# Attention of a hybrid encoder layer as a longer software pipeline, with half of the sample units transposed on TensorE

## The chip, the cores and the metric

The kernel runs on one core of one Trainium2 chip. The metric is the device time of one execution in microseconds (us). Engines: PE is TensorE (matmuls; PEld its weight loads), DVE is VectorE, ACT is ScalarE, POOL is GpSimd, SP is SyncE, which only issues DMAs here.

## The reference, cut to what matters

One encoder layer is applied to two token groups (256 prompt and 1024 sample tokens) that share their weights: a mixer of grouped-query attention and a gated linear recurrence (HGRN2), then cross-attention to a memory, then an MLP. The change touches the attention of the mixer alone. T is 256 or 1024, there are 8 query heads on 2 key/value heads, 64 numbers each:

```python
def blocked_gqa_attention(q, k, v):          # q (B,T,8,64), k and v (B,T,2,64)
    ...
    def attend(qblk):                        # one block of 128 queries
        s = jnp.einsum('bkgqd,bksd->bkgqs', qblk, kh).astype(jnp.float32) * scale
        p = jax.nn.softmax(s, axis=-1).astype(vh.dtype)
        return jnp.einsum('bkgqs,bksd->bkgqd', p, vh)
...
merged = jax.nn.sigmoid(gate_a) * (o_a @ w_pa) + jax.nn.sigmoid(gate_b) * (o_b @ w_pb)
return merged @ w_out                        # then layer norm, cross-attention, MLP
```

## The kernel before

The phases follow one another: keys and values of the memory, the recurrence (`hgrn`), the projections `qkv`, `attention`, and then `back` for each half of the tokens, which begins with the merge of the two branches and needs the attention's output. To keep precision every fp32 operand of a matmul is a high and a low part, so that a product takes two or three matmuls.

`attention` works in 68 **units**, in this order: 64 of the sample group (one head, 128 queries, 1024 keys each; two units in a row, `qt` 0 and 1, make up one head's 256 queries), then 4 of the prompt group (four heads, 128 queries, 256 keys each). Inside the loop over `x` (a **step**) one operation of several units is written out, and within `tc.manual_schedule` PE, ACT and DVE run their instructions in just the order in which the code gives them. POOL and SP get theirs from a scheduler. For one sample unit:

- `scores`: four matmuls (L437, L438) into a PSUM tile `S`, of which there are two;
- `row_max` (L443, DVE), then `exps` (L451, ACT), which writes the unnormalised weights `pr` (three buffers in turn) and their sums `sm`;
- `recip` (L456 and L457, DVE): 1/sum, with a factor `PS`;
- the weights must be normalised, split into two f16 parts, and transposed, so that keys lie on partitions. For two units in three the DMA transposes: `dma_hi` (L464, ACT) writes the high part into `p16`, `dma_lo` (L469, DVE) the low part, and SP issues a transposing DMA (L471). Every third sample unit (`on_pe`, 21 of the 64) goes by TensorE instead: POOL normalises (L561), `pe_turn` makes eight transposes into the one PSUM tile `T` (L477), ACT copies the high part from it (L570), DVE subtracts for the low part (L571);
- `weigh`: 16 matmuls with the values for two units of a head (L490, called PV below), in two pieces of eight, then the **eviction** of the PSUM tile `of` by ACT into `oev` (L494), and a DMA to DRAM. One piece is issued a step, `PVLAG` steps after the unit.

Into the same loop a **filler** is woven: 144 pieces of three matmuls (L116 to L118) that project gates needed later, two or three a step. Eight pieces fill one `of` tile, which ACT copies to `gev` (L630) and POOL's queue stores. PV and filler share the two `of` tiles (pool `psV`). The filler's weights are loaded by SP, and split by ACT (L86, "weight cast" below) and POOL (L87).

The prompt units have no PE transposes. Behind the last unit come the last PVs, their stores (`oa_d<-oev`, two `oev` buffers), the loads `y<-oa_d` in `back` (L729) and their split (L86), for which the merge's matmuls wait. Meanwhile PE does matmuls of `back` that need no attention (`a<-act,w`).

Of the kernel before, what the change touches and what calls it, by code (L numbers as in the profile page):

```python
# [10 lines left out]
F32 = mybir.dt.float32  # L11
# [3 lines left out]
AF = mybir.ActivationFunctionType  # L15
ALU = mybir.AluOpType
# [4 lines left out]
P = 128  # L21
# [5 lines left out]
KT = D // P  # L27
HD = 64
# [10 lines left out]
GRP = T // 2  # L39
GCH = [(0, 256), (256, 384)]  # L40
# [18 lines left out]
W8E = (0, 1, 0, 1)  # L59
PORD = 64  # L60
PVS = 1
PVLAG = 5
PEVERY = 3
VS = 1024.0
PS = 32768.0


class Kern:
# [340 lines left out]
    def attention(self, ap, psS, psT, psV, fills):  # L409
        nc = self.nc  # L410
        SC = 256
        aw = self.t(self.actp, [P, 10240], F32, "act")
        cnt = {"pt": 0, "pr": 0}

        def new_pt(m):
            i = cnt["pt"] % 4
            cnt["pt"] += 1
            return aw[:, i * 2048:(i + 1) * 2048].bitcast(F16).rearrange("p (j a s q) -> p j a s q", j=2, a=m, q=SC)

        def new_pr(m):  # L420
            i = cnt["pr"] % 3
            cnt["pr"] += 1
            x = self.t(ap, [P, 1024], F32, "prx", 1) if i == 2 else aw[:, 8192 + i * 1024:9216 + i * 1024]
            return x.rearrange("p (a s) -> p a s", a=m)


        def scores(u):
            si, kv, hs, t0 = u[:4]
            s0, s1 = SEQS[si]
            L = (s1 - s0) * P  # L430
            n = min(512, L)
            S = self.t(psS, [P, 1024], F32, "S")
# [21 lines left out]
        def recip(u, sm):  # L454
            m = len(u[2])
            nc.vector.tensor_scalar(sm[:, :m], sm[:, :m], 1.0 / PS, None, op0=ALU.mult)  # L456
            nc.vector.reciprocal(sm[:, :m], sm[:, :m])  # L457
# [9 lines left out]
        def dma_lo(u, pr, sm, p16, dst):  # L467
            for a in range(len(u[2])):
                nc.vector.scalar_tensor_tensor(p16[:, 1, a], pr[:, a], sm[:, a:a + 1], p16[:, 0, a],  # L469
                                               op0=ALU.mult, op1=ALU.subtract)  # L470
            nc.sync.dma_start_transpose(out=dst.rearrange("p j a s q -> p (j a s) q"), in_=p16.rearrange("p j a s -> p (j a s)"))  # L471


        def pe_turn(pr):
            pt = self.t(psT, [P, 8, P], F32, "T")
            for j in range(8):
                nc.tensor.transpose(pt[:, j], pr[:, 0, j * P:(j + 1) * P], self.ident)  # L477
            return pt

        def weigh(si, h0, c0, pts):  # L480

            s0, s1 = SEQS[si]
# [12 lines left out]
            if m == 2:  # L495
                for j in range(2):
                    nc.sync.dma_start(self.oa_d[j, h0 // 2, :, :, c0:c0 + SC].rearrange("h d t -> d h t"), os_[j * HD:(j + 1) * HD])
            else:
                nc.sync.dma_start(self.oa_d[:, h0 // 2, h0 % 2, :, c0:c0 + SC], os_[:, 0])

        units = []

# [15 lines left out]
        pvs = []  # L518

        def slot(x):  # L520
            u = units[x]
            if u[4] == 0:
                u[5][0] = new_pt(len(u[2]))
            return u[5][0][:, :, :, :, u[4] * P:(u[4] + 1) * P]

        def close(x):
            si, kv, hs, t0, qt, pts, c0 = units[x]
            if qt:
                k = min(2, len(hs))
                pvs.extend((x, weigh(si, hs[a], c0, [pts[0][:, :, a + y] for y in range(k)])) for a in range(0, len(hs), k))  # L530

        def step_pv(x, k):
            while k > 0 and pvs and pvs[0][0] <= x - PVLAG:
                if next(pvs[0][1], 0) == 0:
                    pvs.pop(0)
                else:
                    k -= 1

        keys = [("wga" if g[0] == 0 else "wgb", g[1]) for g in fills]

        def feed():
            for i, g in enumerate(fills):
                if i + 1 < len(fills):
                    self.w_ahead(keys[i + 1])
                yield from self.gate(*g, psV, "of", self.evp)
# [5 lines left out]
        for x in range(n + PVLAG + 3):  # L551
# [4 lines left out]
            y, z = x - 1, x - 2  # L556
            if 0 <= y < n:
                recip(units[y], R[y][1])
                if on_pe[y]:
                    pr, sm = R[y]  # L560
                    nc.gpsimd.tensor_scalar(pr, pr, sm[:, 0:1], None, op0=ALU.mult)  # L561
            if 0 <= z < n and not on_pe[z]:
                dma_lo(units[z], *R.pop(z), H.pop(z), slot(z))
                close(z)
            if x + 1 < n:
                M[x + 1] = row_max(units[x + 1], S[x + 1])
            if 0 <= z < n and on_pe[z]:
                pt = pe_turn(R.pop(z)[0])
                dst = slot(z)
                nc.scalar.copy(dst[:, 0, 0], pt)  # L570
                nc.vector.tensor_tensor(dst[:, 1, 0], pt, dst[:, 0, 0], op=ALU.subtract)  # L571
                close(z)
            if 0 <= y < n and not on_pe[y]:
                H[y] = dma_hi(units[y], *R[y])
# [4 lines left out]
        assert not pvs  # L579
        for _ in filler:  # L580
            pass

    def memproj(self, mp, psF):
        nc, a = self.nc, self.a
# [33 lines left out]
    def gate(self, j, db, groups, pool, tag, evp):  # L618

        nc = self.nc  # L620
        w = self.w("wga" if j == 0 else "wgb", db)
        for g in groups:
            for c0, n in GCH:
                ps = self.t(pool, [P, 512], F32, tag)
                for k in range(KT):
                    self.mm_t(ps[:, :n], w, self.xT[g], c0, n, kts=(k,), first=k == 0, last=k == KT - 1)
                    if k < KT - 1:
                        yield 1
                ev = self.t(evp, [P, 384], F32, "gev", 3)
# [464 lines left out]
```

## Time and profile before

| what | value |
|---|---|
| time, median of 3 runs | 2538.37 us (2536.22 to 2541.3) |
| the profiled execution's own time | 2541.5 us |
| its span, first to last instruction | 2539.4 us |
| PE busy in the span | 2414.5 us (95%) |
| DVE, ACT, POOL busy | 1336.6 (53%), 852.0 (34%), 528.0 us (21%) |
| granted TensorE clock, mean (1 is full speed, 2.4 GHz) | 0.987 |

The span is 2.1 us shorter than the execution's own time. Busy shares are means over phases with different limits; matmul ends are modelled, so a busy PE need not be at its peak.

### The profile page before, as it was taken

How to read it: one execution, taken by the hardware profiler on the slowest of the kernel's cores; microseconds unless marked ns; L12 is line 12 of the kernel's file. 1: busy time of each engine (PE TensorE's matmuls, PEld its weight loads, DVE VectorE, ACT ScalarE, POOL GpSimd, SP SyncE). 2: the span in 40 equal slices, each digit the busy share in tenths (PEclk: the TensorE clock that was granted, in tenths of full speed). 3: DMA queues.
4: the chain of work that ended last, by engine and by line, in shares of the span. 5: the costliest groups of instructions: out<-in, count | busy, mean ns of one | idle time of the engine just before them, and what ended most of it. 6: DMA issues, size and time to landing. Idle time of an engine off the chain costs nothing.

```text
span 2539.4 us, 35916 instructions
## 1 busy us (share of the span) xinstructions
PE 2414.5 (95%) x14852; PEld 2235.0 (88%) x14852; DVE 1336.6 (53%) x2085; ACT 852.0 (34%) x1429; POOL 528.0 (21%) x408
## 2 busy tenths in 40 slices
PE   7999999999987877899999999999999999999998
PEld 6899999999966667879899999999999889999996
DVE  5136654565866663763654444458344565444435
ACT  4222222223466655423332222232323423222220
POOL 4621222214543442231200000004322210000000
PEclk9999999999999999999999999999999999999999
DMA  7710111112266766624322222235323413222211
GB/s 266 174 42 31 42 40 36 44 32 63 64 116 130 138 130 163 212 88 149 108 77 82 84 89 72 88 98 193 126 85 133 158 42 109 74 75 75 75 59 50
DMA packets 176482, 248.48 MB, mean 98 GB/s; under 512 B 108416, under 2 KB 121744, under 8 KB 175296
## 3 DMA queue, kind: packets, MB, share of 16 engines
q1 hardware_dynamic: 156416, 199.65, 28.3%
q0 software_dynamic: 19904, 46.55, 5.7%
q8 instruction: 116, 1.90, 0.3%
q14 instruction: 46, 0.38, 0.0%
HBM read 192.82 MB, written 28.05 MB: 87 GB/s over the span
## 4 chain that ended last, share of the span: by engine, by line
PE 71%; DVE 7%; ACT 4%; DMA 4%; issue 2%; POOL 1%; SPq 0%; POOLq 0%; DVEq 0%; ACTq 0%
PE a L117 9%; PE a L118 9%; PE a L116 9%; PE a L127 8%; PE a L128 8%; PE a L129 8%; PE pj L118 2%; PE pj L116 2%; PE pj L117 2%; PE lv L236 2%; PE of L490 2%; PE of L116 1%; PE of L118 1%; PE of L117 1%; ACT p L464 1%
## 5 line engine op out<-in xcount | busy, mean ns | idle before, releaser
L116 PE MATMUL a<-act,w 128*128 128x384 f32 (+1 forms) x1664 | 514.0, 310 | 9.4 <-ACT act L86 9.4
L117 PE MATMUL a<-act,w 128*128 128x384 f32 (+1 forms) x1664 | 515.3, 310 | 0.1
L118 PE MATMUL a<-act,w 128*128 128x384 f32 (+1 forms) x1664 | 514.5, 310 | 0.0
L87 POOL TENSOR_TENSOR w<-raw,w 128x1024 fp32r<-128x1024 f32 (+2 forms) x100 | 251.5, 2518 | 574.6 <-ACT w L86 573.9
L116 PEld LDWEIGHTS a<-act,w 128*128 128x128 f32 x1664 | 316.3, 190 | 10.6 <-ACT act L86 10.0
L117 PEld LDWEIGHTS a<-act,w 128*128 128x128 f32 x1664 | 316.4, 190 | 1.1 <-DVE act L87 0.5
L118 PEld LDWEIGHTS a<-act,w 128*128 128x128 f32 x1664 | 316.2, 190 | 0.0
L86 ACT CAST w<-raw 128x1024 fp32r<-128x1024 f32 (+1 forms) x210 | 218.5, 1042 | 249.3 <-PE a L129 163.9
L116 PE MATMUL pj<-act,w 128*128 128x384 f32 (+2 forms) x688 | 221.3, 322 | 9.2 <-ACT act L86 6.1
L117 PE MATMUL pj<-act,w 128*128 128x384 f32 (+2 forms) x688 | 221.9, 323 | 5.5 <-DVE act L87 5.5
L133 POOL TENSOR_SCALAR rs<-mv 128x1 f32<-128x1 f32 x30 | 17.1, 569 | 999.4 <-DVE mv L641 999.2
L118 PE MATMUL pj<-act,w 128*128 128x384 f32 (+2 forms) x688 | 220.2, 322 | 3.3 <-POOL w L87 3.3
L912 DVE SCALAR_TENSOR_TENSOR y<-y,a 128x512 f32<-128x512 f32 x160 | 109.7, 686 | 166.2 <-PE a L129 165.6
L127 PE MATMUL a<-w,act 128*128 128x512 f32 x480 | 188.0, 392 | 2.4 <-ACT act L86 2.4
L128 PE MATMUL a<-w,act 128*128 128x512 f32 x480 | 188.4, 393 | 0.9 <-DVE w L87 0.9
L127 PE MATMUL a<-act,act 128*128 128x512 f32 x480 | 186.9, 390 | 1.3 <-ACT act L86 1.3
L129 PE MATMUL a<-w,act 128*128 128x512 f32 x480 | 187.8, 391 | 0.0
L129 PE MATMUL a<-act,act 128*128 128x512 f32 x480 | 187.1, 390 | 0.0
L128 PE MATMUL a<-act,act 128*128 128x512 f32 x480 | 187.1, 390 | 0.0
L87 DVE TENSOR_TENSOR w<-raw,w 128x1024 fp32r<-128x1024 f32 x110 | 134.6, 1224 | 62.5 <-ACT w L86 62.5
L900 DVE TENSOR_TENSOR sg<-sg 128x256 f32<-128x256 f32 (+1 forms) x128 | 62.7, 491 | 169.1 <-ACT sg L899 164.6
L86 ACT CAST act<-raw 128x1024 fp32r<-128x1024 f32 (+2 forms) x84 | 76.2, 918 | 216.0 <-PE a L129 148.9
(212 smaller groups left out, 4804.7 us busy)
## 6 DMA issues: line engine op xcount, KB each, us to landing
raw<-in_wup_dram SPq DMA_DIRECT2D x64, 512.0 KB
raw<-in_wdn_dram SPq DMA_DIRECT2D x64, 512.0 KB
raw<-in_wh_dram SPq DMA_DIRECT2D x16, 512.0 KB
raw<-in_wpab_dram SPq DMA_DIRECT2D x16, 512.0 KB
raw<-in_wout_dram SPq DMA_DIRECT2D x16, 512.0 KB
raw<-in_wxq_dram SPq DMA_DIRECT2D x16, 512.0 KB
act<-k_d POOLq DMA_DIRECT2D x8, 1024.0 KB, 6.1
act<-v_d POOLq DMA_DIRECT2D x16, 512.0 KB, 6.2
```

The costliest lines, as they stand in the source:

```text
L86: nc.scalar.copy(hi, src)
L87: (eng or nc.vector).tensor_tensor(lo, src, hi.bitcast(F32), op=ALU.subtract)
L116: nc.tensor.matmul(ps, wh, xh, start=st, stop=False)
L117: nc.tensor.matmul(ps, wh, xl, start=False, stop=False)
L118: nc.tensor.matmul(ps, wl, xh, start=False, stop=en)
L127: nc.tensor.matmul(ps, xh, wh, start=st, stop=False)
L128: nc.tensor.matmul(ps, xh, wl, start=False, stop=False)
L129: nc.tensor.matmul(ps, xl, wh, start=False, stop=en)
L236: nc.tensor.matmul(ps[:, c - b0], ka[:, c * P:(c + 1) * P], view(qp, c), start=True, stop=True)
L490: nc.tensor.matmul(ov[:, i], vv, pt[:, x, st], start=st == 0 and x == 0, stop=st == ns - 1 and x == 1)
L900: nc.vector.tensor_tensor(r[:, :n], r[:, :n], r[:, :n], op=ALU.mult)
L912: nc.vector.scalar_tensor_tensor(y[:, i, c], y[:, i, c], ALPHA if fb == 0 else 1.0, ps, op0=ALU.mult, op1=ALU.add)
```

## The change

The pipeline of a unit becomes longer: each operation stands a step or more behind the one that feeds it. With z a unit's number, before: exponentials in step z, reciprocal and `dma_hi` in z+1, `dma_lo` or all of transposes, copy and subtraction in z+2, PV from about z+5. After: reciprocal z+1, `dma_hi` or the transposes z+2, `dma_lo` or the high copy z+3, the subtraction z+4, and PV two steps behind the later of a head's two units. `PEVERY` 2 makes every odd sample unit one for PE: 32 in place of 21. DVE normalises these (L586 of the changed kernel) where POOL did; for the DMA's units POOL now multiplies the 128 reciprocals by `PS` (L588). `pr` has four buffers. Evictions are put on a list (`later`) and issued by `flush` at the start of the next step. A prompt head gets an `of` tile and a store of its own (eight in place of four). `gev` has two buffers in place of three, in `gate` too, which other phases call.

```diff
-PVLAG = 5
-PEVERY = 3
+PVLAG = 2
+PEVERY = 2
...
         def new_pr(m):
-            i = cnt["pr"] % 3
+            i = cnt["pr"] % 4
             cnt["pr"] += 1
-            x = self.t(ap, [P, 1024], F32, "prx", 1) if i == 2 else aw[:, 8192 + i * 1024:9216 + i * 1024]
+            x = self.t(ap, [P, 1024], F32, "prx", 2) if i >= 2 else aw[:, 8192 + i * 1024:9216 + i * 1024]
...
-                    if st % 4 == 3:
+                    if st % 4 == 3 and (i < m - 1 or st < ns - 1):
                         yield 1
-            os_ = self.t(ap, [P, 2, SC], F32, "oev", 2)[:, :m]
-            nc.scalar.activation(os_, ov, AF.Copy, scale=self.vd[:, kv, si:si + 1])
...
+            def out():
+                os_ = self.t(ap, [P, m, SC], F32, "oev", 2)
+                nc.scalar.activation(os_, ov, AF.Copy, scale=self.vd[:, kv, si:si + 1])
...
+            later.append(out)
...
-            if qt:
-                k = min(2, len(hs))
-                pvs.extend((x, weigh(si, hs[a], c0, [pts[0][:, :, a + y] for y in range(k)])) for a in range(0, len(hs), k))
+            pts["n"] = pts.get("n", 0) + 1
+            pts["at"] = max(pts.get("at", 0), at)
+            if pts["n"] == 2:
+                pvs.extend((pts["at"], weigh(si, h, c0, [pts[0][:, :, a]])) for a, h in enumerate(hs))
...
+                        def out(ps=ps, k=k, dst=self.g_d[j, db, :, g * GRP + c0:g * GRP + c0 + k]):
+                            ev = self.t(self.evp, [P, 384], F32, "gev", 2)[:, :k]
+                            nc.scalar.copy(ev, ps)
+                            nc.gpsimd.dma_start(dst, ev)
+                        later.append(out)
...
+        for x in range(n + PVLAG + 6):
+            flush()
             if x < n:
                 R[x] = exps(units[x], S.pop(x), M.pop(x))
             if x + 1 < n:
                 S[x + 1] = scores(units[x + 1])
...
+            z = x - 4
+            if z in turned:
+                dst = slot(z)
+                nc.vector.tensor_tensor(dst[:, 1, 0], turned.pop(z), dst[:, 0, 0], op=ALU.subtract)
+                close(z, x)
+            y = x - 1
             if 0 <= y < n:
...
+                nc.vector.reciprocal(sm[:, :m], sm[:, :m])
                 if on_pe[y]:
...
-                    nc.gpsimd.tensor_scalar(pr, pr, sm[:, 0:1], None, op0=ALU.mult)
...
+                    nc.vector.tensor_scalar(pr, pr, sm[:, 0:1], PS, op0=ALU.mult, op1=ALU.mult)
+                else:
+                    nc.gpsimd.tensor_scalar(sm[:, :m], sm[:, :m], PS, None, op0=ALU.mult)
+            z = x - 3
+            if z in H:
+                dma_lo(units[z], *R.pop(z), H.pop(z), slot(z), nc.gpsimd if False else nc.vector)
+                close(z, x + 1)
+            if z in turned:
+                nc.scalar.copy(slot(z)[:, 0, 0], turned[z])
+            z = x - 2
+            if 0 <= z < n:
+                if on_pe[z]:
+                    turned[z] = pe_turn(R.pop(z)[0])
+                else:
+                    H[z] = dma_hi(units[z], *R[z])
             if x + 1 < n:
                 M[x + 1] = row_max(units[x + 1], S[x + 1])
```

What stands on the engines changes as follows. ACT in the middle of the sample units, before: each row is an instruction, its output and inputs by their tiles (`p` is `p16`, `act` holds most `pr` buffers and the transposed weights).

```order
L451 ACTIVATE act_6303,sm_6812<-S_6777,mx_6787 128x1024
L570 CAST act_6303<-T_6823 128x8x128
L464 ACTIVATE p_794_6834<-act_6303,sm_6775 128x1024
L494 ACTIVATE oev_6836<-of_6760,vd 128x256
L451 ACTIVATE prx_6858,sm_6857<-S_6814,mx_6821 128x1024
L464 ACTIVATE p_801_6871<-act_6303,sm_6812 128x1024
L451 ACTIVATE act_6303,sm_6887<-S_6860,mx_6869 128x1024
L494 ACTIVATE oev_6901<-of_6839,vd 128x256
```

And ACT there after the change:

```order
L491 ACTIVATE oev_6996<-of_6952,vd 128x256
L451 ACTIVATE act_6303,sm_6999<-S_6970,mx_6980 128x1024
L451 ACTIVATE prx_7038,sm_7037<-S_7001,mx_7020 128x1024
L594 CAST act_6303<-T_7011 128x8x128
L459 ACTIVATE p_830_7048<-act_6303,sm_6968 128x1024
L491 ACTIVATE oev_7066<-of_7022,vd 128x256
```

The cycle is now two steps long: an eviction and exponentials in an odd step, exponentials, high copy from `T` and `dma_hi` in an even one; the eviction stands ahead of its step's exponentials, where it stood behind all of its step's work.

DVE in the same place, before (a unit of the DMA, then one of PE, then one of the DMA):

```order
L443 TENSOR_REDUCE mx_7007<-S_6997 128x1
L456 TENSOR_SCALAR sm_6995<-sm_6995 128x1
L457 RECIPROCAL sm_6995<-sm_6995 128x1
L443 TENSOR_REDUCE mx_7032<-S_7025 128x1
L571 TENSOR_TENSOR act_6303<-T_7034,act_6303 128x8x128
L456 TENSOR_SCALAR sm_7023<-sm_7023 128x1
L457 RECIPROCAL sm_7023<-sm_7023 128x1
L469 SCALAR_TENSOR_TENSOR p_828_7045<-act_6303,sm_6995,p_828_7045 128x1024
```

And DVE after, one cycle of two steps:

```order
L443 TENSOR_REDUCE mx_7050<-S_7040 128x1
L578 TENSOR_TENSOR act_6303<-T_7011,act_6303 128x8x128
L584 RECIPROCAL sm_7037<-sm_7037 128x1
L464 SCALAR_TENSOR_TENSOR p_830_7048<-act_6303,sm_6968,p_830_7048 128x1024
L443 TENSOR_REDUCE mx_7094<-S_7075 128x1
L584 RECIPROCAL sm_7072<-sm_7072 128x1
L586 TENSOR_SCALAR prx_7073<-prx_7073,sm_7072 128x1024
```

The subtraction and `dma_lo` now share the odd step; the even one holds the normalising that POOL did.

ACT behind the last unit, after the change (the prompt's evictions from `oev_8849` on; `y` are tiles that `back` loads):

```order
L491 ACTIVATE oev_8849<-of_8833,vd 128x256
L86 CAST act_8910<-y_8912 128x1280 x2
L491 ACTIVATE oev_8852<-of_8838,vd 128x256
L491 ACTIVATE oev_8875<-of_8855,vd 128x256
L86 CAST w_9232<-raw_9230 128x1024
L491 ACTIVATE oev_8878<-of_8860,vd 128x256
L491 ACTIVATE oev_8881<-of_8865,vd 128x256
L491 ACTIVATE oev_8884<-of_8870,vd 128x256
```

Eight prompt evictions of 256 columns stand here (six are shown), where four of 512 stood.

## Rows read from the trace of the kernel before

**Rows 1.** Busy time in three stretches: sample units, prompt units, behind the last unit

```profile
core 0: us, PE busy (x) PEld busy (x) DVE busy (x) ACT busy (x) POOL busy (x), PEclk, DMA share, GB/s
702.25:961.36 259.11, 204.19 (x1277) 171.34 (x1276) 168.93 (x252) 165.15 (x246) 111.39 (x49) 0.95 0.67 131
961.36:976.65 15.29, 12.28 (x74) 10.82 (x73) 8.40 (x16) 10.16 (x33) 0.78 (x2) 0.78 0.52 92
976.65:1021.68 45.03, 31.44 (x223) 29.39 (x223) 12.06 (x23) 20.33 (x39) 9.10 (x6) 0.96 0.81 221
```

**Rows 2.** Waits from 702 to 966 us: total us, times, longest

```profile
PE of L490 <- ACT oev L494: 40.7, 20, 3.2
...
PE of L116 <- ACT gev L630: 4.4, 7, 1.2
PE of L116 <- ACT oev L494: 4.2, 3, 1.6
...
PE T L477 <- POOL prx L561: 3.2, 2, 1.7
```

**Rows 3.** Timeline from 907.5 us: start, duration, instruction [idle before it]

```profile
909.13 1.15 ACT L464 ACTIVATE p<-act,sm 128x1024 f16<-128x1024 f32 x1
...
910.18 0.47 ACT L494 ACTIVATE oev<-of,vd 128x256 f32<-128x256 f32 x1
...
910.70 1.03 PE L490 MATMUL of<-act,vn 128*128 128x256 f16 x8 [2.51 <-ACT oev L494]
```

**Rows 4.** Timeline of PE over one step with transposes

```profile
847.52 0.40 PE L437 MATMUL S<-kh,act 128*128 128x512 f32 x1
...
848.45 1.04 PE L477 MATMUL T<-ident,prx 128*128 128x128 f32 x8
849.32 1.04 PE L490 MATMUL of<-act,vn 128*128 128x256 f16 x8
...
851.26 0.40 PE L437 MATMUL S<-kh,act 128*128 128x512 f32 x1
```

**Rows 5.** Groups by line, 700 to 1008 us: busy, mean ns | idle before

```profile
L443 DVE TENSOR_REDUCE mx<-S 128x1 f32<-128x1024 f32 x64 | 78.1, 1222 | 66.6 <-PE S L438 66.6
...
L469 DVE SCALAR_TENSOR_TENSOR p<-act,sm,p 128x1024 f16<-128x1024 f32 x43 | 58.2, 1352 | 1.1 <-ACT p L464 1.1
...
L451 ACT ACTIVATE act<-S,mx 128x1024 f32<-128x1024 f32 x43 | 48.1, 1119 | 38.0 <-DVE sm L456 36.6 <-DVE sm L457 0.7 <-DVE mx L443 0.6
...
L571 DVE TENSOR_TENSOR act<-T,act 128x1024 f16<-128x1024 f32 x21 | 25.7, 1225 | 19.0 <-ACT act L570 19.0
...
L570 ACT CAST act<-T 128x1024 f16<-128x1024 f32 x21 | 21.3, 1012 | 24.7 <-PE T L477 24.7
...
L86 ACT CAST w<-raw 128x1024 fp32r<-128x1024 f32 x13 | 13.5, 1046 | 0.1
...
L451 ACT ACTIVATION_READ_ACCUMULATOR act<-S,mx 128x1 f32 x55 | 11.0, 199 | 0.0
L457 DVE RECIPROCAL sm<-sm 128x1 f32<-128x1 f32 x64 | 10.5, 164 | 2.2
```

**Rows 6.** The same view of DVE, 590 to 640 us: scaling the values

```profile
L348 DVE TENSOR_SCALAR act<-act,vi 128x1024 f32<-128x1024 f32 x1 | 0.8, 755 | 0.0
```

**Rows 7.** Instructions of line 185: shortest, median and longest in ns

```profile
L185 DVE TENSOR_SCALAR act<-act x8: 827/1706/2819, 123.6 to 498.8; 128x1280 f32<-128x1280 f32 x8
```

**Rows 8.** Timeline of POOL and DVE from 928 us

```profile
928.32 2.35 POOL L87 TENSOR_TENSOR w<-raw,w 128x1024 fp32r<-128x1024 f32 x1 [5.39 <-ACT w L86]
...
929.33 2.42 DVE L469 SCALAR_TENSOR_TENSOR p<-act,sm,p 128x1024 f16<-128x1024 f32 x1 [0.22 <-ACT p L464]
```

**Rows 9.** The page's group of POOL's smallest multiplications

```profile
L133 POOL TENSOR_SCALAR rs<-mv 128x1 f32<-128x1 f32 x30 | 17.1, 569 | 999.4 <-DVE mv L641 999.2
```

**Rows 10.** Timeline of PE behind the last unit

```profile
995.88 1.05 PE L490 MATMUL of<-act,vn 128*128 128x256 f16 x8 [2.17 <-DMA act<-p]
...
1021.68 1.43 PE L116 MATMUL a<-act,w 128*128 128x256 f32 x4 [7.49 <-ACT act L86]
```

**Rows 11.** Timeline of ACT behind the last unit

```profile
999.68 0.69 ACT L494 ACTIVATE oev<-of,vd 128x512 f32<-128x512 f32 x1 [5.00 <-DMA oa_d<-oev]
```

More of the change, by code (lines that the diff above doesn't have):

```diff
@@ L452, in exps @@
             return pr, sm
[L454 to L457, printed above, removed]
         def dma_hi(u, pr, sm):
@@ L465, in dma_hi, with dma_lo @@
             return p16
-        def dma_lo(u, pr, sm, p16, dst):
+        def dma_lo(u, pr, sm, p16, dst, eng):
             for a in range(len(u[2])):
-                nc.vector.scalar_tensor_tensor(p16[:, 1, a], pr[:, a], sm[:, a:a + 1], p16[:, 0, a],
+                eng.scalar_tensor_tensor(p16[:, 1, a], pr[:, a], sm[:, a:a + 1], p16[:, 0, a],
                                                op0=ALU.mult, op1=ALU.subtract)
@@ L490, in weigh @@
                         nc.tensor.matmul(ov[:, i], vv, pt[:, x, st], start=st == 0 and x == 0, stop=st == ns - 1 and x == 1)
-                    if st % 4 == 3:
+                    if st % 4 == 3 and (i < m - 1 or st < ns - 1):
                         yield 1
-            os_ = self.t(ap, [P, 2, SC], F32, "oev", 2)[:, :m]
-            nc.scalar.activation(os_, ov, AF.Copy, scale=self.vd[:, kv, si:si + 1])
[L495 to L499, printed above, removed]
+            def out():
+                os_ = self.t(ap, [P, m, SC], F32, "oev", 2)
+                nc.scalar.activation(os_, ov, AF.Copy, scale=self.vd[:, kv, si:si + 1])
+                if m == 2:
+                    for j in range(2):
+                        nc.sync.dma_start(self.oa_d[j, h0 // 2, :, :, c0:c0 + SC].rearrange("h d t -> d h t"), os_[j * HD:(j + 1) * HD])
+                else:
+                    nc.sync.dma_start(self.oa_d[:, h0 // 2, h0 % 2, :, c0:c0 + SC], os_[:, 0])
+            later.append(out)
         units = []
@@ L532, in step_pv @@
         def step_pv(x, k):
-            while k > 0 and pvs and pvs[0][0] <= x - PVLAG:
+            while k > 0 and pvs and pvs[0][0] + PVLAG <= x:
                 if next(pvs[0][1], 0) == 0:
                     pvs.pop(0)
-                else:
-                    k -= 1
+                k -= 1
         keys = [("wga" if g[0] == 0 else "wgb", g[1]) for g in fills]
         def feed():
-            for i, g in enumerate(fills):
+            for i, (j, db, groups) in enumerate(fills):
                 if i + 1 < len(fills):
@@ L544, in feed @@
                     self.w_ahead(keys[i + 1])
-                yield from self.gate(*g, psV, "of", self.evp)
+                w = self.w(*keys[i])
+                for g in groups:
+                    for c0, k in GCH:
+                        ps = self.t(psV, [P, 512], F32, "of")[:, :k]
+                        for kt in range(KT):
+                            self.mm_t(ps, w, self.xT[g], c0, k, kts=(kt,), first=kt == 0, last=kt == KT - 1)
+                            if kt < KT - 1:
+                                yield 1
+                        def out(ps=ps, k=k, dst=self.g_d[j, db, :, g * GRP + c0:g * GRP + c0 + k]):
[3 more added lines that the diff above has]
+                        later.append(out)
+                        yield 1
@@ L546, in attention, with flush @@
+        def flush():
+            while later:
+                later.pop(0)()
         self.w_ahead(keys[0])
@@ L550, in attention @@
         M[0] = row_max(units[0], S[0])
-        for x in range(n + PVLAG + 3):
+        turned = {}
+        for x in range(n + PVLAG + 6):
+            flush()
             if x < n:
@@ L555, in attention @@
                 S[x + 1] = scores(units[x + 1])
-            y, z = x - 1, x - 2
+            z = x - 4
[4 more added lines that the diff above has]
+            y = x - 1
             if 0 <= y < n:
-                recip(units[y], R[y][1])
+                pr, sm = R[y]
+                m = len(units[y][2])
+                nc.vector.reciprocal(sm[:, :m], sm[:, :m])
                 if on_pe[y]:
-                    pr, sm = R[y]
-                    nc.gpsimd.tensor_scalar(pr, pr, sm[:, 0:1], None, op0=ALU.mult)
-            if 0 <= z < n and not on_pe[z]:
-                dma_lo(units[z], *R.pop(z), H.pop(z), slot(z))
-                close(z)
+                    nc.vector.tensor_scalar(pr, pr, sm[:, 0:1], PS, op0=ALU.mult, op1=ALU.mult)
[11 more added lines that the diff above has]
+                    turned[z] = pe_turn(R.pop(z)[0])
+                else:
+                    H[z] = dma_hi(units[z], *R[z])
             if x + 1 < n:
                 M[x + 1] = row_max(units[x + 1], S[x + 1])
[L567 to L574, printed above, removed]
             step_pv(x, PVS if x < n else 9)
@@ L578, in attention @@
                 fed += 1
-        assert not pvs
         for _ in filler:
             pass
+        flush()
+        assert not pvs
     def memproj(self, mp, psF):
@@ L628, in gate @@
                         yield 1
-                ev = self.t(evp, [P, 384], F32, "gev", 3)
+                ev = self.t(evp, [P, 384], F32, "gev", 2)
                 nc.scalar.copy(ev[:, :n], ps[:, :n])
```

6 lines of the change are left out of this document (3 added, 3 removed).

## Prediction

> **What bounds the kernel now.** I first cut the attention into three stretches by the starts of row maxima [rows 1]: the 64 sample units from the first row maximum to that of the first prompt unit, 259.1 us; the prompt units up to the last row maximum, 15.3 us; and from there to the point where PE gets the merge's first operand, 45.0 us. The reader should look at PE: in the first stretch it is busy for 204.2 of 259.1 us, so 54.9 us are idle, and no other engine is busier than 169 us. A step takes 259.1/64 = 4.05 us, of which PE works 3.19. No engine is the bound there; PE, the nearest to it, waits.
>
> The view of waits then says for whom [rows 2]: 40.7 us, 20 times, the first matmul of a PV waited until ACT had evicted the previous head's tile, and 4.2 us the filler did the same. That is 44.9 of the 54.9 us. The filler waited 4.4 us for its own eviction and the transposes 3.2 us for POOL's normalising. One of the long waits is shown [rows 3]: ACT did `dma_hi` of 1.15 us, then the eviction of 0.47 us, and PE's PV began 0.05 us after that, having stood for 2.51 us. The eviction itself is short; it comes late because the same step's exponentials, copy and `dma_hi` stand ahead of it in ACT's fixed order.
>
> **The change part by part.** *The eviction's place.* In the order of ACT the eviction of a finished head now stands ahead of the exponentials of the next step, and PE asks for that tile only after that step's scores and, in odd steps, after the transposes: 0.93 and 0.87 us of PE work [rows 4] that formerly had no such work of ACT to outlast. I count all 44.9 us as removed. The filler's eviction stands in effect where it stood (behind `dma_hi`), so its 4.4 us stay.
>
> *More transposes.* Eleven more units go by PE. One group of eight occupies PE from 848.45 to 849.32, 0.87 us [rows 4]; 11 x 0.87 = 9.6 us more of PE. That PE now asks for them a full step after DVE normalised removes the 3.2 us [rows 2]. So by PE alone the stretch would take 259.1 - 44.9 - 3.2 + 9.6 = 220.6 us.
>
> *A ring through DVE and ACT.* The instructions that must follow each other once in two steps are row maximum 1.222, exponentials 1.119, reading of the sums 0.199, high copy from `T` 1.012, subtraction 1.225, reciprocal 0.164, `dma_lo` 1.352, and again a row maximum [rows 5]: 6.29 us, with three hand-overs between engines at the 0.05 us of rows 3 it is 6.44. Over 32 pairs 206.2 us. Into ACT's order come 11 weight casts of 1.05 us in that stretch [rows 5], 11.5 us, none of which PE sees directly, but all of which may stand on the ring: 217.7 us. So two chains of nearly one length, 218 and 221 us, run side by side and each will now and then hold the other up. I take 226 us, 5 us above PE's sum; the bounds are 214 (204.2 + 9.6, all idle time gone) and 237 us (half of the 44.9 us come back). The stretch falls by 33 us.
>
> *Normalising on DVE.* The nearest row is DVE's scaling of the values by a number per partition, 0.755 us for the same 128x1024 [rows 6]. DVE then has per pair 2 x 1.222 + 2 x 0.164 + 1.352 + 1.225 + 0.755 = 6.10 us, below 6.9 (PE, 220.6/32), and the addition lies in the even step, outside the ring. If that cover were gone it would cost 32 x 0.755 = 24 us. But another DVE multiplication of this kind took 0.83 to 2.82 us [rows 7], and `dma_lo` took 2.42 us where it usually takes 1.35, while POOL was subtracting from 928.32 on [rows 8, 5]: something is shared. The Trainium skill, SBUF — State Buffer, "Who interferes with whom", says that GpSimd and a VectorE instruction that is in a two-port mode or reads two SBUF operands exclude each other for a whole instruction; it speaks against putting this work on DVE, and the rows agree with it. Taken from the rows alone, the upper bound for one normalising is 2.82, but POOL's own normalising disappears from the kernel and its long subtractions are few (one per weight cast, 11), so I take 0.755 and, for the range, 11 x 2.06 = 23 us more on DVE, mostly covered by the 0.8 us a pair that DVE has free.
>
> *POOL's small multiplication.* `dma_hi` now waits for POOL's product; the nearest row is 0.57 us [rows 9], and `dma_hi` comes a step and a half after the reciprocal, some 5 us. It stands on POOL behind a weight subtraction (2.35 us, [rows 8]) at worst. Bounds: nothing, and 0.57 us in each of 32 pairs, 18 us. I take nothing. The DVE factor multiplication that goes away is inside the sums above.
>
> *Buffers and transposing DMAs.* Four `pr` buffers and fewer transposing DMAs (36 in place of 47) only loosen; from `dma_lo` to PV pass about three and a half steps of 3.5 us, as three of 4.05 us before, so I count nothing. `gev` with two buffers could hold a gate elsewhere; the bound is the 4.4 us that these evictions cost now. I take zero.
>
> *Prompt units.* PE is busy 12.3 of 15.3 us [rows 1] and has the same work; the idle time mostly goes: -3 us.
>
> *Behind the last unit.* The last PV waits for the transposing DMAs [rows 10], which are as many and as large for the last five units; they start at the same step. After them ACT has eight evictions through two `oev` buffers where four stood, and one eviction has waited 5.00 us for the store that frees its buffer [rows 11]. PE stands 7.49 us for the result [rows 10], so this part counts. Bounds: 0, and four more such waits, 20 us. PE has work of its own there and the DMA feeds the prompt heads in two lots, so I take one wait less a little, +4 us.
>
> *Sum.* -33 - 3 + 4 = -32 us on the profiled execution's own 2541.5 us (2.1 us of it outside the span): 2509.5 us. It lay 3.1 us above the median of the three runs, so I predict 2506 us.
>
> **The rivals.** *Ring held by POOL, 2516 us:* the small product takes what POOL and DVE share just before `dma_lo`, which follows the same reciprocal. Then 0.57 us is added to each ring: 32 x 7.01 + 11.5 = 236 us, a fall of 23 in place of 33. For it: rows 8; against: DVE's instruction is already queued when POOL has yet to be woken. *The waits only move, 2540 us:* an eviction at the head of ACT's step must wait for the PE matmuls that end the step before, and the exponentials queue behind it, then the row of the ring. There are 28 PV and 16 filler evictions in that stretch; at about 0.8 us each this eats 35 us and leaves nothing. For it: the evictions of the filler are already late in rows 2; against: PV's last piece ends ahead of the filler's pieces, so ACT seldom waits for it. *Slower, 2576 us:* DVE becomes the bound. With normalising at 2.82 [rows 7] and `dma_lo` at 2.42 us [rows 8] every time, DVE's pair is 9.24 us, more than today's 8.10 (259.1/32), which is the point from which it decides; 32 x 9.24 = 296 us, +37 in place of -33. Against it: both were seen only beside POOL instructions of over 2 us, which become rare.
>
> **How the numbers follow.** I give my forecast 0.60 (its own range 2490 to 2522, from the bounds 214 us of the body and 20 us behind it), the held ring 0.20, moved waits 0.10, the DVE bound 0.10. Changes below 0.2% (5 us) can't be told from none in this kernel. Faster: 0.60 + 0.20 + 0.04 of the moved waits = 0.84; same 0.05; slower 0.11. The range reaches from 2488, where PE has no idle time in the body, to 2530, where half of the waits come back and the tail costs its 20 us.
>
> **What the profile after would show.** Right: sample units in 220 to 230 us, PE's waits for `oev` below 10 us, DVE's normalising near 0.76 us, the idle time of POOL's `prx` group gone, the tail within 45 to 50 us. The eviction step is wrong if `of` is still waited for on ACT; the ring if row maxima wait for anything but scores; the tail if evictions wait for stores more than twice. The forecast as a whole fails if DVE's pair exceeds 7 us or if ACT waits for PE at the head of its steps.

## The result and the profile after

The changed kernel takes 2506.69 us (median of 4 runs, 2505.13 to 2509.4) against 2539.84 us before: ratio 0.9872, 95% interval 0.9855 to 0.9889. The prediction was 2506 us, range 2488 to 2530. The total agrees, but two of its terms were off by some 15 and 20 us in opposite directions.

The windows of the changed kernel, cut at the same three places as [rows 1] (columns as there):

```profile
695.50:907.26 211.76, 199.74 (x1357) 170.59 (x1356) 184.81 (x219) 160.41 (x245) 67.94 (x60) 1.00 0.71 131
907.26:920.03 12.77, 10.98 (x77) 10.13 (x75) 7.05 (x11) 10.13 (x32) 1.99 (x4) 0.87 0.72 136
920.03:989.80 69.77, 40.57 (x255) 36.97 (x254) 17.44 (x28) 23.43 (x47) 9.39 (x8) 0.80 0.58 158
```

The sample units take 211.8 us in place of 259.1, the prompt units 12.8 in place of 15.3, and the stretch behind the last row maximum has grown from 45.0 to 69.8 us. PE is busy for 199.7 of the 211.8 us, so 12 us are idle where 54.9 were, and its granted clock there rose from 0.95 to 1.00.

The view of waits of the sample units, for PE (total us, times, longest), answers [rows 2]:

```profile
PE T L472 <- DVE sm L584: 5.6, 8, 1.2
...
PE of L116 <- ACT oev L491: 2.9, 3, 1.4
...
PE of L116 <- ACT gev L555: 2.1, 4, 0.6
```

The 40.7 us for which PVs waited for the previous head's eviction have no row any more. Of 44.9 us of waits for evictions 2.9 are left.

The rest of the comparison goes from the last row maximum to the program's end, because the parts of that stretch shift against each other: 1562.8 us before (2539.4 - 976.65) and 1585.8 after (2505.8 - 920.03), 23.0 us longer. The timeline of ACT there shows why; it answers [rows 11]:

```profile
936.65 0.47 ACT L491 ACTIVATE oev<-of,vd 128x256 f32<-128x256 f32 x1 [1.43 <-DMA oa_d<-oev]
...
942.02 0.47 ACT L491 ACTIVATE oev<-of,vd 128x256 f32<-128x256 f32 x1 [3.96 <-DMA oa_d<-oev]
947.82 0.47 ACT L491 ACTIVATE oev<-of,vd 128x256 f32<-128x256 f32 x1 [5.32 <-DMA oa_d<-oev]
...
974.17 0.47 ACT L491 ACTIVATE oev<-of,vd 128x256 f32<-128x256 f32 x1 [9.16 <-DMA oa_d<-oev]
```

Eight evictions of 0.47 us each stood in a chain with stores that must land before one of the two `oev` buffers is free. The view of waits from 920 to 990 us sums it up, and shows what it costs PE:

```profile
ACT oev L491 <- DMA oa_d<-oev: 29.0, 8, 9.2
...
PE a L116 <- ACT sg L732: 14.4, 1, 14.4
...
PE of L485 <- ACT oev L491: 11.1, 4, 4.3
```

The chain of work over this stretch (shares of it by line) puts more than half on the stores:

```profile
by line: DMA oa_d<-oev 59.8%; DMA act<-p 7.1%; DMA y<-oa_d 7.1%; ACT oev L491 2.9%; issue 2.4%; PE of L485 2.4%; DVE y L759 2.0%; DVE act L87 2.0%; ACT p L459 1.9%; SPq L758 1.7%; ACT act L86 1.7%; PE of L116 1.7%; PE of L117 1.5%; PE of L1
```

The spans differ by 33.6 us (2539.4 and 2505.8): -47.3 in the sample units, -2.5 in the prompt units, +23.0 behind them, and -6.8 because attention began at 695.45 us in place of 702.25. What runs ahead of attention is written alike in both kernels but for `gev`'s buffers, and in the profiles of the experiments below its first row maximum starts anywhere from 692.6 to 702.9 us, in changed kernels (701.55 in e4, 702.87 in e7) as late as before. In these three late profiles the granted clock is below 1.00 somewhere in the first 50 us (0.87 in the first 25 us before), in all others it is 1.00 there. I take this part for the scatter between executions, not for an effect of the change.

### The profile page after: what moved, and what is told of

Its sections match the earlier page's. It is cut to its first block, busy times and chain, and to the rows that moved or that the text cites. A ratio compares the mean times of both kernels' runs of the same rounds, so it can differ in the third digit from the quotient of the medians.

```text
span 2505.8 us, 36016 instructions
## 1 busy us (share of the span) xinstructions
PE 2411.3 (96%) x14940; PEld 2235.2 (89%) x14940; DVE 1350.6 (54%) x2049; ACT 849.9 (34%) x1433; POOL 487.4 (19%) x423
## 4 chain that ended last, share of the span: by engine, by line
PE 72%; DVE 8%; DMA 5%; ACT 2%; issue 1%; POOL 0%; SPq 0%; POOLq 0%; DVEq 0%; ACTq 0%
PE a L117 9%; PE a L118 9%; PE a L116 9%; PE a L127 8%; PE a L128 8%; PE a L129 8%; PE pj L118 2%; PE pj L116 2%; PE pj L117 2%; PE lv L236 2%; DMA oa_d<-oev 2%; PE of L485 1%; PE of L116 1%; PE of L118 1%; PE of L117 1%
## 5 line engine op out<-in xcount | busy, mean ns | idle before, releaser
L116 PE MATMUL a<-act,w 128*128 128x384 f32 (+1 forms) x1664 | 515.1, 310 | 19.7 <-ACT sg L732 14.4
L117 PE MATMUL pj<-act,w 128*128 128x384 f32 (+2 forms) x688 | 220.6, 321 | 3.0 <-DVE act L87 3.0
```

Of the source, the lines that this page charges most:

```text
L116: nc.tensor.matmul(ps, wh, xh, start=st, stop=False)
L117: nc.tensor.matmul(ps, wh, xl, start=False, stop=False)
```

## The experiments

Each time is the median of 4 runs (e9: 7, e11: 10). The ratio is to the kernel before as it ran beside each group (medians 2536.95 us for e1 to e4, 2536.13 for e5 to e8, 2538.89 for e9 to e12). "Sample units" is again the time from the first sample unit's row maximum to the first prompt unit's, and "the rest" that from the last row maximum to the end of the span; both are read from one profile of each kernel. Four kernels that share the code of the sample units (changed, e1, e2, e7) have 211.8 to 211.9 us there.

| kernel | time, us | ratio to before [95%] | sample units, us | the rest, us |
|---|---|---|---|---|
| before | 2539.84 | 1 | 259.1 | 1562.8 |
| changed | 2506.69 | 0.9872 [0.9855, 0.9889] | 211.8 | 1585.8 |
| e1_slots8 | 2496.55 | 0.9846 [0.9818, 0.9873] | 211.9 | 1573.9 |
| e2_pairs2 | 2479.77 | 0.9771 [0.9751, 0.9792] | 211.9 | 1562.0 |
| e3_before_evict | 2499.89 | 0.9850 [0.9830, 0.9869] | 230.6 | 1564.3 |
| e4_late | 2510.14 | 0.9893 [0.9867, 0.9919] | 214.7 | 1587.7 |
| e5_third | 2505.66 | 0.9874 [0.9859, 0.9889] | 239.4 | 1561.9 |
| e6_pool | 2481.80 | 0.9785 [0.9761, 0.9809] | 209.1 | 1561.3 |
| e7_slots8_poolq | 2487.67 | 0.9800 [0.9774, 0.9826] | 211.8 | 1564.6 |
| e8_dve_ps | 2486.08 | 0.9805 [0.9782, 0.9828] | 213.1 | 1564.6 |
| e9_before_half | 2530.67 | 0.9953 [0.9933, 0.9973] | 250.6 | 1562.1 |
| e10_before_half_evict | 2514.61 | 0.9897 [0.9876, 0.9919] | 240.5 | 1560.7 |
| e11_late_third | 2543.95 | 1.0016 [1.0000, 1.0032] | 248.9 | 1586.7 |
| e12_third_p16x4 | 2489.57 | 0.9788 [0.9760, 0.9816] | 222.8 | 1564.0 |

### Behind the last unit: e1, e2, e7

**e1_slots8** is the changed kernel with a place of its own for each of the eight prompt evictions, in a slot for transposed weights that is used up by then:

```diff
-                os_ = self.t(ap, [P, m, SC], F32, "oev", 2)
+                if si:
+                    os_ = self.t(ap, [P, m, SC], F32, "oev", 2)
+                else:
+                    i = cnt["ev"] = cnt.get("ev", -1) + 1
+                    os_ = aw[:, 4096 + i * SC:4096 + (i + 1) * SC].rearrange("p (h t) -> p h t", h=1)
```

> The changed kernel, but each of the eight prompt evictions gets 256 columns of its own in a buffer of transposed weights that no one needs any more, so none waits for a store to free a buffer. Theory (in the changed kernel the stretch behind the last row maximum grew from 45.0 to 69.8 us because eight stores of 5 to 11 us follow one another through two buffers): that stretch falls to 45 to 50 us, the time to 2482 to 2488 us, the sample units stay at 212 us. Rival (the stretch is long because the transposing DMAs and PE's other work end late, and the waits for stores only fill it): below 5 us gained, 2502 to 2507 us.

No eviction waits for a store now, and yet only half of the 23 us came back: 2496.55 us. The timeline of SP in e1 shows what is left:

```profile
953.29 10.93 SPq L500 DMA_DIRECT2D oa_d<-act  x4
964.35 5.49 SPq L762 DMA_DIRECT2D y<-oa_d  x2
970.26 0.34 SPq L93 DMA_DIRECT2D raw<-in_wpab_dram  x1
970.71 0.51 SPq L500 DMA_DIRECT2D oa_d<-act  x1
981.67 0.88 SPq L762 DMA_DIRECT2D y<-oa_d  x2
```

In SP's order the last store (970.71) stands behind the two loads of the merge's first half, which themselves wait for earlier stores to land; the eviction it stores had ended at 961.7. The loads of the second half begin 11 us behind it. Five of the evictions (951 to 961 us) stand behind casts of the merge in ACT's order.

**e2_pairs2** is the changed kernel with the prompt heads weighed and evicted in pairs, as before: four evictions of 512 columns, through two places of that slot in turn.

```diff
-                pvs.extend((pts["at"], weigh(si, h, c0, [pts[0][:, :, a]])) for a, h in enumerate(hs))
+                k = min(2, len(hs))
+                pvs.extend((pts["at"], weigh(si, hs[a], c0, [pts[0][:, :, a + y] for y in range(k)])) for a in range(0, len(hs), k))
```

> The changed kernel, but the prompt heads are weighed and evicted in pairs, four evictions of 512 columns with two stores each, through two buffers in turn, as in the kernel before. Theory (number of turns through two buffers sets the length): the stretch behind the last row maximum comes back to 45 to 55 us, the time is 2485 to 2495 us. Rival (the longer pipeline itself, whose last unit is weighed later, makes the stretch long): the stretch stays at 65 to 70 us, the time at 2503 to 2507 us.

It took 2479.77 us, less than the theory allowed, and the rest is back at 1562.0 us, so the pipeline's length costs nothing there: the 23 us come from the eight single evictions and the way in which their stores went out. The stores themselves are as many and as large in all three kernels, eight of 128 KB for the prompt: before the change each of the four evictions had two, so it is the evictions that doubled. This is also the fastest version, 27 us ahead of the changed kernel. SP's timeline of e2 has two stores for each eviction, in two lots, and the last is issued by 949.4 us, some 21 us before e1's:

```profile
941.00 2.62 SPq L498 DMA_DIRECT2D oa_d<-act  x4
...
945.00 1.09 SPq L763 DMA_DIRECT2D y<-oa_d  x2
...
946.79 2.62 SPq L498 DMA_DIRECT2D oa_d<-act  x4
...
959.55 0.89 SPq L763 DMA_DIRECT2D y<-oa_d  x2
```

**e7_slots8_poolq** is e1 with these eight stores issued by POOL (`nc.gpsimd` in place of `nc.sync` for the prompt).

> The kernel of e1_slots8 (2496.55 us; 67.1 us from the last row maximum to the last addition of the merge's operand) with the eight stores of the prompt heads issued by POOL. Theory: the last store was issued on SP at 970.7, 9.5 us after its eviction had ended at 961.2, because the loads of the first half stand ahead of it in SP's order; on POOL it goes out at once: the tail 56 to 60 us, time 2485 to 2490 us. Rival: the evictions stand late in ACT's order, behind casts that wait for loads, and the store's landing is what remains: the tail 64 to 68 us, time 2493 to 2499 us.

2487.67 us; from the last row maximum to the last addition of the merge's operand passed 58.9 us, as the theory had it. So of the 23 us, about 12 were the two buffers (e1), and most of the remaining 11 the stores' place on SP (e7: 9.3 more, from 1573.9 to 1564.6 us). e7 moves all eight stores; that it was the last one that counted is read from e1's timeline.

### The sample units: eviction, share and pipeline length

The change makes three alterations there: the eviction's place, the length of the pipeline, and TensorE's share of the units. All eight combinations were run. With the pipeline go the normalising (to DVE in the longer one), the buffers of `pr` and `gev`, and the place of the filler's eviction. Sample units in us:

| pipeline | share on TensorE | eviction late | eviction early |
|---|---|---|---|
| old | a third | 259.1 (before) | 230.6 (e3) |
| old | a half | 250.6 (e9) | 240.5 (e10) |
| longer | a third | 248.9 (e11) | 239.4 (e5) |
| longer | a half | 214.7 (e4) | 211.8 (changed) |

**e3_before_evict** is the kernel before with the eviction issued in the step of the last PV piece:

```diff
-                    if st % 4 == 3:
+                    if st % 4 == 3 and (i < m - 1 or st < ns - 1):
                         yield 1
...
                     pvs.pop(0)
-                else:
-                    k -= 1
+                k -= 1
```

> The kernel before, with one part of the change: the eviction of a finished head is issued in the step of its last piece and not in the next, and the next head begins a step later. All else, the order of the pipeline, a third of the units on PE, normalising on POOL, stays. Theory (44.9 us of PE's waits in the sample units were for this eviction's place): the sample units fall from 259.1 to 215 to 230 us, the time to 2500 to 2512 us. Rival (the place of the operations on DVE and ACT within the step, and not the eviction, set the pace; the waits would move to the next link): sample units 245 to 260 us, time 2525 to 2540 us.

2499.89 us, at the lower end of the theory's range, with 230.6 us of sample units, 0.6 above theirs: 28.5 us less there from this alone. The old pipeline with this one part, and without the eight evictions at its end, is no slower than the whole change (2506.69 us).

**e4_late** undoes the same lines in the changed kernel and calls `out()` directly in place of `later.append(out)`.

> The changed kernel, with that part undone: the eviction of a head is issued a step after its last piece, behind that step's other work on ACT, and the next head begins in the same step, as before. Theory: PE's waits for the eviction come back, 30 to 45 us of them, the sample units take 240 to 257 us, the time is 2535 to 2552 us. Rival (the longer pipeline has given ACT and DVE enough lead that the eviction's place does not matter): sample units 212 to 220 us, time 2505 to 2515 us.

Here my theory fell: 2510.14 us, and PVs waited for evictions 2.1 us in all. With the longer pipeline and half of the units on TensorE, a late eviction costs 2.9 us (214.7 against 211.8), not the 44.9 us of waits that it explained before.

**e5_third** is e2 with `PEVERY = 3`.

> The kernel of e2_pairs2 (2479.77 us; sample units 211.9 us) with every third unit on TensorE, as before the change, in place of every second. Theory: in the sample units PE is nearly without idle time (199.7 of 211.8 us in the profile after), so PE's work sets the length; 11 groups of eight transposes fewer at about 0.85 us take 9 us away: sample units 201 to 205 us, time 2469 to 2474 us. Rival: the 11 more transposing DMAs come late for the PVs or hold the ring of ACT and DVE: sample units 212 to 220 us, time 2480 to 2489 us.

Both failed: I had expected a faster kernel, and the sample units took 239.4 us, 27.5 more, above even the rival's bound. The view of waits of e5 over its sample units names what is late:

```profile
ACT p L459 <- DMA act<-p: 29.4, 12, 6.0
DVE p L464 <- ACT p L459: 21.5, 11, 5.2
...
ACT oev L495 <- PE of L485: 18.5, 8, 4.8
...
PE of L485 <- ACT oev L495: 13.0, 6, 3.9
```

`dma_hi` (L459) waits for a `p16` buffer, of which there are two and which a transposing DMA holds until it has landed. In the changed kernel the same row is 0.7 us, once. The window of that stretch (columns as in [rows 1]) has a granted clock of 0.93, against 1.00. Of the 27.5 us, 22.5 are more idle time of PE (34.5 in place of 12.0), and the other 5 are busy time, although PE has fewer transposes to do:

```profile
694.06:933.46 239.40, 204.86 (x1276) 172.12 (x1274) 172.25 (x210) 163.28 (x244) 59.43 (x70) 0.93 0.78 138
```

**e12_third_p16x4** gives e5 four `p16` buffers, two of them in place of the fourth slot for transposed weights:

```diff
-            i = cnt["pt"] % 4
+            i = cnt["pt"] % 3
...
-            p16 = self.t(ap, [P, 2048], F16, "p16", 2).rearrange("p (j a s) -> p j a s", j=2, a=m)
+            i = cnt["p16"] = cnt.get("p16", -1) + 1
+            p16 = self.t(ap, [P, 2048], F16, "p16", 2) if i % 4 < 2 else aw[:, 6144 + i % 2 * 1024:7168 + i % 2 * 1024].bitcast(F16)
+            p16 = p16.rearrange("p (j a s) -> p j a s", j=2, a=m)
```

> The kernel of e5_third (2505.66 us, sample units 239.4 us) with four p16 buffers in place of two, the two more in the place of the fourth slot for transposed weights, of which three remain. Theory: the buffers are what ACT waits for (29.4 us), so the wait goes: sample units 208 to 220 us, time 2474 to 2487 us. Rival: the transposing DMAs themselves can't keep the pace of two in three units, and more buffers only move the wait to the PVs: sample units 230 to 242 us, time 2496 to 2509 us.

222.8 us: between the two, nearer to the theory. ACT's wait for `p16` has no row left, and 16.6 of the 27.5 us came back. What remains was not taken apart: part may be the rival's, as the waits in e12's sample units have this row now, which the changed kernel doesn't, and part may be the slot that was taken away:

```profile
PE of L487 <- DMA act<-act: 5.1, 4, 3.3
```

**e9_before_half** and **e10_before_half_evict** are before and e3 with `PEVERY = 2`.

> The kernel before with every second unit on TensorE and nothing else changed. Theory: the late eviction keeps PE waiting whatever the share: sample units 248 to 262 us (259.1 before), time 2526 to 2542 us. Rival: the share alone brings most of the gain, because fewer transposing DMAs loosen the whole step: sample units 215 to 238 us, time 2492 to 2517 us.

> The kernel of e3_before_evict (2499.89 us, sample units 230.6 us) with every second unit on TensorE. Theory: with the evictions early, what was left there is ACT's wait for the two p16 buffers that transposing DMAs hold (20.8 us), and the share removes it without a longer pipeline: sample units 211 to 220 us, time 2481 to 2490 us. Rival: the longer pipeline is needed for that too: sample units 226 to 236 us, time 2495 to 2506 us.

e9 went by the theory (2530.67 us, sample units 250.6, PVs waiting 24.1 us for evictions). e10 went by neither: 240.5 us is above both ranges, and slower than e3 with its third. The view of waits of e10 over its sample units shows a row of engines that wait for each other:

```profile
DVE act L570 <- ACT act L569: 51.6, 30, 3.2
...
ACT act L569 <- PE T L477: 41.4, 30, 2.3
...
PE T L477 <- POOL act L560: 18.5, 17, 2.2
```

In the old pipeline transposes (L477), ACT's high copy (L569) and DVE's subtraction (L570) stand in one step, so that each engine waits for the one ahead, in 30 units in place of 20. The wait for `p16` is gone there, as expected, but this one takes its place. The longest member of the row is POOL's normalising (L560), which heads the chain of work over e10's sample units, and a part of that chain:

```profile
by line: POOL act L560 27.7%; PE T L477 13.3%; DVE act L570 11.7%; POOL prx L560 11.1%; ACT act L569 9.9%; issue 8.1%; POOL w L87 2.3%; PE of L490 2.2%; PE S L438 1.9%; PE S L437 1.9%; PE of L116 1.8%; DVE sm L457 1.7%; PE of L118 1.2%; PE 
```

```profile
803.64 3.71 POOL act L560
...
811.25 3.73 POOL prx L560
```

Between these two lines stand eight transposes, copy, subtraction, and the next reciprocal, which follows the subtraction in DVE's order: a ring of 7.61 us for two units, and 240.5/32 is 7.52. So normalising is 38.8% of that chain. The longer pipeline puts transposes, copy and subtraction in steps of their own (in the changed kernel the wait for the copy is 1.7 us in all), and it normalises in less time. Which of the two broke the ring is not shown: the old pipeline with a quicker normalising was not run.

**e11_late_third** is e4 with `PEVERY = 3`.

> The kernel of e4_late (2510.14 us, sample units 214.7 us) with every third unit on TensorE: of the change only the longer pipeline and the normalising on DVE are left in the sample units. Theory: ACT waits for the p16 buffers as in e5_third: sample units 234 to 248 us, time 2529 to 2545 us. Rival: the wait in e5_third came from the early eviction, which stands on SP between the transposing DMAs: sample units 213 to 226 us, time 2508 to 2522 us.

The time (2543.95 us) lies where the theory had it (the sample units 0.9 us above), but not for its reason. ACT waits 4.6 us for `p16`; the PVs' waits for the eviction are back:

```profile
PE of L485 <- ACT oev L491: 29.3, 17, 3.9
...
ACT p L459 <- DMA act<-p: 4.6, 5, 3.0
```

So at a third the eviction's place matters in the longer pipeline too. Why a half removes its cost was not taken apart.

### The normalising and POOL's product: e6, e8

**e6_pool** is e2 with the normalising back on POOL:

```diff
-                    nc.vector.tensor_scalar(pr, pr, sm[:, 0:1], PS, op0=ALU.mult, op1=ALU.mult)
+                    nc.gpsimd.tensor_scalar(pr, pr, sm[:, 0:1], PS, op0=ALU.mult, op1=ALU.mult)
```

> The kernel of e2_pairs2 with the normalising for TensorE's units given back to POOL. Theory: DVE does not set the length (184.8 of 211.8 us busy), and the transposes come a step after the normalising on either engine: sample units 210 to 214 us, time 2477 to 2483 us. Rival: moving it to DVE was worth the 3.2 us or more for which the transposes waited on POOL, now for 32 units: sample units 217 to 226 us, time 2485 to 2495 us.

2481.8 us with 209.1 us of sample units, 0.9 below the theory's range: the same time as e2, though DVE is busy for 153 us there in place of 185. DVE is not the bound, and in the longer pipeline this normalising may stand on either engine. But it is not the instruction of the kernel before, which had one multiplication where e6 has two. The lines of both, shortest, median and longest in ns, first the kernel before, then e6:

```profile
L561 POOL TENSOR_SCALAR prx<-prx,sm x21: 2842/3711/3813, 710.8 to 957.8; 128x1024 f32<-128x1024 f32 x21
L591 POOL TENSOR_SCALAR act<-act,sm x16: 1112/1127/1133, 700.4 to 900.1; 128x1024 f32<-128x1024 f32 x16
```

What the slow one would cost the longer pipeline, no run shows.

**e8_dve_ps** is e2 with the product of 1/sum and `PS` on DVE, where it takes 0.154 us:

```diff
-                    nc.gpsimd.tensor_scalar(sm[:, :m], sm[:, :m], PS, None, op0=ALU.mult)
+                    nc.vector.tensor_scalar(sm[:, :m], sm[:, :m], PS, None, op0=ALU.mult)
```

> The kernel of e2_pairs2 with the small product of 1/sum and PS on DVE in place of POOL. Theory: POOL's product (0.98 us in the profile after) lies in the step and a half before dma_hi and holds nothing: sample units 210 to 214 us, time 2477 to 2483 us. Rival, the ring held by POOL: without it the sample units take 204 to 208 us, time 2471 to 2476 us.

The sample units took 213.1 us, not 204 to 208, so POOL's product holds nothing; the rival is out. The time of 2486.08 us was above the theory's range by 3 us; a profile each doesn't settle whether that is an effect.

## Why the prediction came out right, and where it did not

**The size.** On the profiled executions' own times (2541.5 and 2507.55 us) the kernel fell by 34 us where 32 were predicted. The terms were -33, -3 and +4; measured are -47.3, -2.5 and +23.0, and 6.8 us of scatter ahead of attention. The errors of the first and third nearly cancel, and that is luck: the stretch behind the last unit went beyond the bound that the prediction gave it (20 us), the sample units beyond theirs (214 us), in opposite directions.

**The eviction's place: counted rightly, not the only way.** "I count all 44.9 us as removed" holds: 2.9 us are left. That the place of the eviction removes them is shown in the old pipeline (e3, -28.5 us). But e4 shows that the other two alterations together remove them as well (-44.4 us), and then the place is worth 2.9. The prediction credited one cause with what either can do. The 3.2 us of transposes that wait for the normalising did not go, as it had them: they are 5.6 us now, on DVE.

**More transposes: the sign was wrong.** The step costed eleven more units on PE at +9.6 us and said of the fewer transposing DMAs "only loosen ... so I count nothing". With the longer pipeline the larger share is worth -27.6 us (e5 against the changed kernel, 239.4 and 211.8) or -34.2 with late evictions (e11, e4). With two units in three on the DMA, ACT has no wait for the two `p16` buffers at the old pace of 4.05 us a step, 4.6 us in e11 (3.89 us a step), 29.4 in e5 (3.74) and 20.8 in e3 (3.60): at the faster pace two are not enough. e12 shows the buffers to be the larger part of it. What I left out was to ask whether the DMA's units keep the new pace.

**The body's size.** I predicted 226 us, of which PE's work was 213.8 (204.2 + 9.6) and 12.2 idle. Measured are 199.7 of work and 12.0 idle: the idle time was right, and PE's work was mis-sized. Its granted clock rose from 0.95 to 1.00; by an estimate from these rows 204.2 x 0.95 + 9.6 = 203.6 us, so about 10 of the 14 us are the clock, and the other 4 are open. The stated lower bound of 214 us had been worked out at the old clock and was passed for that reason. The upper bound of 237 us does not come out of PE's sum, where half of the waits gives 220.6 + 22.5 = 243 us; nothing measured hangs on it. The second chain, the ring of 217.7 us with eleven casts on it, was too long as well: the stretch is shorter than it.

**Normalising.** The line's instructions in the changed kernel, shortest, median and longest in ns:

```profile
L586 DVE TENSOR_SCALAR act<-act,sm x16: 752/755/2628, 700.5 to 901.4; 128x1024 f32<-128x1024 f32 x16
```

The median is the 0.755 us of [rows 6]; the mean is 1.10 (1.142 and 1.055 us for its two forms), because a few take up to 2.6 us, beside POOL's weight subtractions as in [rows 8]. Over 32 units this is 11 us more on DVE, half of the 23 that I had allowed, and it is covered: DVE works 184.81/32 = 5.78 us a pair, below the 6.9 that I allowed it.

**The tail: the mechanism was named, its size was not taken.** The prediction saw "eight evictions through two `oev` buffers where four stood" and one store of 5 us, gave 20 us as the upper bound and took +4, since PE has work of its own. It was 23.0 us. All eight evictions stood for a store, PE ran out of work (14.4 us in one piece), and the bound left out the last store's place on SP behind the merge's loads (e1, e7). That the transposing DMAs "start at the same step" was wrong too: `dma_lo`, which they follow, stands a step later in the longer pipeline. e2, with the rest back at 1562.0 us, shows no cost of that. The criterion "if evictions wait for stores more than twice" did show it.

**The rivals.** The ring held by POOL is refuted by e8, and taking nothing for POOL's product was right. Waits that only move: ACT waited 17.0 us for the filler at the head of its steps (28.6 us before, at their end). By the prediction's own sign this would have meant that it fails as a whole; it was no such sign, as PE was not held by it. DVE as the bound: e6 takes 32 us of work from DVE and gains nothing.

## What to carry to other kernels

When a change makes a loop faster, hold each stage that is out of sight against the new pace: here two buffers that a transposing DMA holds were enough at 4.05 us a step and not at 3.6 to 3.7, and the share of the units on TensorE, which looks like a cost, was what let the longer pipeline pay. Hold each member of a ring against it as well: in e10 one slow normalising on POOL headed the chain. A wait that one alteration removes may be removed by another too, so that parts must be tried alone and together before either is credited. At the end of a pipeline little hides the last stores: fewer and larger evictions, through places that need not be waited for, with their stores ahead of the next phase's loads on their queue, gave back 23 us.

## What the runs showed of the hardware

POOL's product of 128 reciprocals (512 for a prompt unit) takes 0.219 us at its shortest and 1.09 us as its median:

```profile
L588 POOL TENSOR_SCALAR sm<-sm x36: 219/1089/1167, 698.2 to 924.3; 128x1 f32<-128x1 f32 x32, 128x4 f32<-128x4 f32 x4
```

The timeline of DVE and POOL in the changed kernel shows it beside `dma_lo`, and then a normalising beside a weight subtraction:

```profile
844.08 1.27 DVE L464 SCALAR_TENSOR_TENSOR p<-prx,sm,p 128x1024 f16<-128x1024 f32 x1
844.32 1.10 POOL L588 TENSOR_SCALAR sm<-sm 128x1 f32<-128x1 f32 x1 [5.63 <-DVE sm L584]
845.46 2.36 POOL L87 TENSOR_TENSOR w<-raw,w 128x1024 fp32r<-128x1024 f32 x1
846.58 1.79 DVE L586 TENSOR_SCALAR act<-act,sm 128x1024 f32<-128x1024 f32 x1
```

The product starts inside `dma_lo` and ends 0.07 us behind it (845.42 and 845.35). The normalising starts inside POOL's subtraction, which ends at 847.82, and ends 0.55 us later, at 848.37. Each looks as if it had stood until the other engine was done. The Trainium skill, SBUF — State Buffer, "Who interferes with whom", says that GpSimd and a VectorE instruction that reads two SBUF operands or runs in a two-port mode exclude each other for a whole instruction; this trace agrees. In which mode the normalising ran no row shows. In this kernel it costs little: e8 without the product on POOL and e6 without the normalising on DVE are no faster than e2.

The other surprise is how long a small store holds its buffer: in the chain of the last eight, evictions of 0.47 us stood up to 9.16 us for stores of 256 columns, and in e1 the loads began 11 us after the store they needed had been issued. And the granted clock of the sample units (1.00 is the level of 2.4 GHz) was 1.00 in the changed kernel, with PE idle for 12 of 211.8 us, 0.95 before (54.9 idle) and 0.93 in e5 and e11 (34.5 and 42.5 idle), but 0.98 in e9 with 41.4 us idle: how long PE stands does not order them by itself.
